# First block rearranged: modulation sums in one PSUM bank, bundled state products, attention in steps between projections

## The chip, the cores and the metric

The kernel runs on one core of a Trainium2 chip, one program, one launch. The metric is the device time of that core in microseconds (us). Five engines work beside each other, each through its own queue in order: TensorE (PE, and PEld for its weight loads), VectorE (DVE), ScalarE (ACT), GpSimd (POOL) and SyncE (SP), which here only issues DMAs. PSUM is the memory that TensorE writes its sums into, in banks of 128 partitions x 512 floats; SBUF is the working memory.

## What is computed

The first block takes x (256 tokens x 1024) through a mixer with two branches and a mixture of experts; a second block of feed-forward layers, a pooling mixer and an attention follows. The change lies in the first block's mixer, and in the first modulation of the second block:

```python
h = rmsnorm(x, g_mix[l])
proj = h @ w_in[l]                      # 1024 x 5376
aq, ak, av, hq, hf_f, hf_b, hi, hg, gate_a, gate_b = jnp.split(proj, SPLIT_POINTS, axis=-1)
attn_o = bidir_gqa(aq, ak, av, q_norm[l], k_norm[l])      # 8 heads of 64, 2 key heads, softmax over 256
hgrn_o = hgrn2_bidir(hq, hf_f, hf_b, hi, hg, lbs_f[l], lbs_b[l], hgrn_norm[l])
merged = (jax.nn.sigmoid(gate_a) * (attn_o @ w_attn_branch[l])
          + jax.nn.sigmoid(gate_b) * (hgrn_o @ w_hgrn_branch[l]))
x = x + merged @ w_out[l]
h = rmsnorm(x, g_ffn[l])
x = x + hier_moe(h, ...)                # 32 experts
...
# hgrn2: q = silu(hq)*scale; f = lb + (1-lb)*sigmoid(z); k = (1-lb)*sigmoid(-z); log_f = log(f)
#   in chunks of 32 tokens, both directions:  S_t = diag(f_t) S_{t-1} + k_t v_t^T ; o_t = S_t^T q_t
# second block: mod = silu(c) @ ada_w[i] + ada_b[i]  gives shift, scale and gate of each sublayer
```

## The kernel before, in words

All data is float32. A large product is made of three matmuls of a shorter float format: each operand is split into a rounded part (`hi`) and the rest (`lo`), and `mm3` (L147 to L150) adds hi*hi, hi*lo and lo*hi into one PSUM bank. `split_w` (L154) splits weights: a cast on ScalarE (L159), a subtraction on VectorE (L160), per 128 x 1024 piece. `gemm_nat` makes a product with tokens on the partitions, in two token blocks `tb` of 128; `gemm_T` (L490) makes it with features on the partitions, in two halves `hp`, and each half is evacuated when its bank is done.

The order of the first block in the source: load x and the gain `g_mix`; normalise a token block (L356), transpose it into `hT` (L360 to L362), project query, key and value (`gemm_nat`); norm and rotary embedding; attention for two token blocks (L430 to L465): per key head g the scores (L440), the row maximum (L443), the exponential with its row sum (L448), transposes (L452), a VectorE copy (L454), the product with v (L458), and at the end the division by the row sum (L463). Then the transposed projections of q and the two gates f (`gemm_T`, evacuated by sigmoids straight from PSUM, L505 to L517), v and the output gate (`gemm_nat`), the recurrence (`hgrn`, from L553: cumulated logarithms, exponentials L569 to L579, products of the chunks, the state chain on VectorE L618, and per state two matmuls into the output, L625), four projections for the branch gates, transposes of both branches' outputs (`to_T`, L347 to L349), the branch products (weights loaded at L664), `w_out`, the router, the experts (L918 on).

The modulation sums of the second block's first two sublayers are made here: `ada_steps` with the engine `pe`, 8 rows of 512 columns. A row's 8 matmuls (L202) put four partial sums on four groups of 32 partitions of a PSUM bank; ScalarE copies the bank (L209), four matmuls against a column of ones add the partials up (L221), VectorE adds the bias (L224).

A scheduler of the framework sets the order on each engine's queue from the program order and its own estimate of durations; `tc.issue_after(x)` keeps a piece behind the instruction x. So the order on a queue is not the source's order. The experts' weights go through SBUF buffers `wgu`, `wdn` (left side) and `xgu`, `xdn` (right side, in pools that take up memory which the first block gives back); SP issues each load when its buffer comes free (L815).

## Time and profile before

| | before |
|---|---|
| device time, median of 3 runs | 1753.44 us (1751.01 to 1757.42) |
| the profiled execution's own time | 1751.05 us |
| its span | 1749.3 us |
| mean granted clock of TensorE | 0.959 |
| TensorE busy | 1569.7 us (90%) |
| VectorE busy | 935.5 us (53%) |
| ScalarE busy | 632.1 us (36%) |
| HBM traffic over the span | 269 GB/s |

The span is the profiled stretch from the first to the last instruction; what lies around it is the difference to the execution's own time. Busy shares are means over the whole span. The first block takes about the first 312 us of it, the experts run to about 756 us, the second block to the end. The granted clock is a share of full speed: 1.00 is the 2.4 GHz level, 0.50 the 1.2 GHz level.

### The profile page before, as it was taken

The page shows a single profiled execution, that of the slowest core. Times are in us where ns is not written, and L with a number is a line of the kernel's source. Part 1 is how long each engine was busy: PE and PEld are TensorE (multiplying, and loading weights), DVE is VectorE, ACT ScalarE, POOL GpSimd, SP SyncE. Part 2 cuts the span into 40 slices and gives each one's busy share as a digit, 9 for nine tenths or more (in the row PEclk, how much of TensorE's full clock was granted, in tenths as well). Part 3 has the DMA queues.
Part 4 walks back from the last instruction along what each step waited for, and adds up shares of the span by engine and source line. Part 5 has one row for each costly group of instructions (what it writes and reads, how often), then busy time and mean ns, then how long its engine had stood idle before and what let it go on. Part 6 is the DMA issues. An engine that isn't in the chain of part 4 may idle for free.

```text
span 1749.3 us, 25202 instructions
## 1 busy us (share of the span) xinstructions
PE 1569.7 (90%) x10307; PEld 1185.4 (68%) x10307; DVE 935.5 (53%) x1620; ACT 632.1 (36%) x1044; POOL 48.9 (3%) x55
## 2 busy tenths in 40 slices
PE   5999998978676778769999899999999999999998
PEld 4875676633223333238999779997999867779997
DVE  4754665312101101037887667778687768765563
ACT  3664444101001000035444444345443456555342
POOL 1100100000000000000000000000000010000000
PEclk8999999899888999889999999999999999999999
DMA  6478475799999999997987467986798565466540
GB/s 199 135 245 295 169 271 213 299 419 420 420 421 377 417 420 421 420 390 266 330 286 259 157 206 252 311 265 209 257 309 282 168 207 178 142 211 216 177 150 25
DMA packets 201727, 472.87 MB, mean 270 GB/s; under 512 B 12712, under 2 KB 105480, under 8 KB 177032
## 3 DMA queue, kind: packets, MB, share of 16 engines
q1 hardware_dynamic: 201608, 471.21, 73.9%
q8 instruction: 83, 1.36, 0.3%
q14 instruction: 36, 0.29, 0.0%
HBM read 470.13 MB, written 1.05 MB: 269 GB/s over the span
## 4 chain that ended last, share of the span: by engine, by line
PE 50%; DMA 10%; DVE 4%; issue 1%; POOL 1%; ACT 1%; SPq 0%; POOLq 0%; DVEq 0%; ACTq 0%
PE ps_g L148 10%; PE ps_g L150 10%; PE ps_g L149 9%; DMA wgu<-in_w_exp_up_dram 5%; PE ps_acc L148 5%; PE ps_acc L150 5%; PE ps_acc L149 5%; DMA xdn<-in_w_exp_down_dram 2%; DMA xgu<-in_w_exp_up_dram 1%; DMA wdn<-in_w_exp_down_dram 1%; PE ps_g L953 1%; POOL rs L137 1%; PE ps_m L221 1%; PE ps_m L1446 1%; DVE rt L1057 1%
## 5 line engine op out<-in xcount | busy, mean ns | idle before, releaser
L148 PE MATMUL ps_g<-hh,hi 128*128 128x256 f32 x1024 | 293.4, 286 | 0.0
L149 PE MATMUL ps_g<-hl,hi 128*128 128x256 f32 x1024 | 289.6, 283 | 0.0
L150 PE MATMUL ps_g<-hh,fl 128*128 128x256 f32 x1024 | 289.1, 282 | 0.0
L1105 DVE TENSOR_TENSOR fl<-fw,hi 128x1024 fp32r<-128x1024 f32 x176 | 211.4, 1219 | 44.2 <-ACT hi L1104 35.2
L1104 ACT CAST hi<-fw 128x1024 fp32r<-128x1024 f32 x176 | 176.8, 1045 | 116.9 <-PE ps_g L149 79.3
L149 PEld LDWEIGHTS ps_g<-hl,hi 128*128 128x128 f32 x1024 | 194.4, 190 | 3.6 <-issue 2.4
L148 PEld LDWEIGHTS ps_g<-hh,hi 128*128 128x128 f32 x1024 | 193.2, 189 | 2.9 <-issue 1.7
L150 PEld LDWEIGHTS ps_g<-hh,fl 128*128 128x128 f32 x1024 | 193.0, 188 | 0.7 <-issue 0.7
L206 DVE SCALAR_TENSOR_TENSOR ev<-ada,condp,ev 128x512 f32<-128x512 f32 x196 | 146.6, 748 | 5.2 <-DMA ada<-in_ada_w_dram 2.2
L150 PE MATMUL ps_acc<-hi,hd 128*128 128x512 f32 x352 | 139.4, 398 | 0.0
L148 PE MATMUL ps_acc<-hi,hd 128*128 128x512 f32 x352 | 138.5, 397 | 0.5 <-ACT hd L1126 0.5
L149 PE MATMUL ps_acc<-fl,hd 128*128 128x512 f32 x352 | 138.3, 394 | 0.0
L918 PE MATMUL ps_g<-wgu,xg 128*32 128x256 f32 x1280 | 91.7, 426 | 41.3 <-DMA wgu<-in_w_exp_up_dram 41.3
L923 DVE TENSOR_TENSOR sq<-sg,ps_g 128x128 f32<-128x128 f32 x32 | 11.9, 373 | 197.1 <-ACT sg L921 197.1
L921 ACT ACTIVATE sg<-ps_g 128x128 f32<-128x128 f32 x32 | 8.9, 278 | 299.8 <-PE ps_g L918 299.8
L160 DVE TENSOR_TENSOR fl<-fw,hi 128x1024 fp32r<-128x1024 f32 x88 | 104.9, 1220 | 20.5 <-ACT hi L159 20.1
L159 ACT CAST hi<-fw 128x1024 fp32r<-128x1024 f32 x88 | 88.6, 1046 | 71.7 <-PE ps_acc L150 69.5
L918 PEld LDWEIGHTS ps_g<-wgu,xg 128*32 128x32 f32 x1280 | 45.7, 121 | 88.0 <-issue 70.5
L148 PE MATMUL ps_g<-hi,hh 128*128 128x512 f32 x240 | 98.0, 409 | 1.4 <-ACT hh L1050 1.2
L150 PE MATMUL ps_g<-hi,hl 128*128 128x512 f32 x240 | 96.7, 404 | 0.0
L953 PE MATMUL ps_g<-wdn,hid 128*32 128x512 f32 x320 | 90.2, 631 | 6.4 <-DVE sq L923 6.4
L957 PE MATMUL ps_acc<-part,ohT 128*128 128x512 f32 x128 | 65.2, 633 | 22.1 <-ACT part L955 12.7
(405 smaller groups left out, 2721.5 us busy)
## 6 DMA issues: line engine op xcount, KB each, us to landing
fw<-in_ffn_w_in_dram SPq DMA_DIRECT2D x88, 1024.0 KB, 7.8
ada<-in_ada_w_dram SPq DMA_DIRECT2D x112, 512.0 KB, 4.8
fw<-in_ffn_w_out_dram SPq DMA_DIRECT2D x44, 1024.0 KB, 6.9
wgu<-in_w_exp_gate_dram SPq DMA_DIRECT2D x40, 1024.0 KB, 19.9
wgu<-in_w_exp_up_dram SPq DMA_DIRECT2D x40, 1024.0 KB, 9.1
wdn<-in_w_exp_down_dram SPq DMA_DIRECT2D x40, 1024.0 KB, 19.8
xgu<-in_w_exp_gate_dram SPq DMA_DIRECT2D x24, 1024.0 KB, 19.9
xgu<-in_w_exp_up_dram SPq DMA_DIRECT2D x24, 1024.0 KB, 7.8
```

What stands on the lines that cost most here:

```text
L137: lead["gp"] = gp.tensor_tensor(out=r, in0=ms, in1=mhalf[:, :n], op=ALU.pow)
L148: pe.matmul(o, ah, bh, start=start, stop=False)
L149: pe.matmul(o, ah, bl, start=False, stop=False)
L150: pe.matmul(o, al, bh, start=False, stop=stop)
L159: lead["hi"] = act.copy(out=hi, in_=w)
L160: lead["lo"] = dve.tensor_tensor(out=lo, in0=w, in1=f32(hi), op=ALU.subtract)
L206: eng.scalar_tensor_tensor(out=o, in0=wk, scalar=ck, in1=o, op0=ALU.mult, op1=ALU.add)
L918: pe.matmul(up[32 * j:32 * j + 32], xg[:, k, s0:s0 + CAP], w[k // 4][:, :, k % 4, j * P:j * P + P], start=k == 0, stop=k == 7)
L953: pe.matmul(o[r_:r_ + 32], hid[i][:, 32 * j:32 * j + 32], wd[i][q][:, jj, c_], start=jj == 0, stop=jj == 1)
L957: pe.matmul(acc[tb][h], ohT[:, tb], part[:, c_], start=e == 0, stop=e == NE - 2)
L1104: act.copy(out=hi, in_=w[:, k_])
L1105: dve.tensor_tensor(out=lo_[:, k_], in0=w[:, k_], in1=f32(hi), op=ALU.subtract)
```

## The change

- The gain `g_mix` is loaded as one row of 4 KB, and two matmuls with a row of ones spread it over the partitions of two PSUM banks; `xn` reads it there.
- The scaling of the router gain `gq` is put inside `issue_after(wr)`, behind the router weights.
- The first modulation sums get a function of their own, `ada_first`: the columns of `condp` are shifted so that row r of eight lands on partition r of each group of 32; all 64 matmuls add into one bank, then one copy, four matmuls with 8 columns (`sel` adds the four groups up), eight additions of the bias.
- Attention is cut into five steps, `attend(tb, g)` and `weigh(tb)`, which `some` issues between the halves of the transposed projections. p is divided by its row sum before it is transposed; the copy of the transposed p is on ScalarE; the product has v as the stationary operand, so that the output comes feature major (`AO`), and no transposes are needed before the branch product. The branch weights of attention come in four loads of 64 partitions.
- The transposed projections are evacuated by plain copies, in the order f forward, q, f backward; sigmoids and logarithms follow from SBUF, the logarithm takes its affine part as scale and bias.
- The state products of the recurrence are issued in two bundles per chain, after the third and the seventh state.
- Buffers: one more `lo`, one more `w2`; `AQ` and `AK` move into `x_sb`, so the pool on the right side shrinks from 24 KB to 20 KB a partition.

The core of the diff:

```diff
-            lo = spl.tile([P, 1024], F32R, tag="lo", name="lo", bufs=4)
+            lo = spl.tile([P, 1024], F32R, tag="lo", name="lo", bufs=5)
...
+    def ada_first(new_w, new_ev):
+        src = io["ada_w_2"][0].rearrange("(k p) n -> p k n", p=P)
+        sums = []
+        def row(r):
+            sl, c, h = r // 4, r // 2 % 2, r % 2
+            n0 = (sl * 3 + c) * D + 512 * h
+            w = [new_w() for _ in range(2)]
+            for q in range(2):
+                sp.dma_start(out=w[q], in_=src[:, 4 * q:4 * q + 4, n0:n0 + 512])
+            if r == 0:
+                sums.append(ps("m", 512))
+            for k in range(8):
+                j = k % 4
+                pe.matmul(sums[0][32 * j:32 * j + 32], condp[:, k, 7 - r:39 - r], w[k // 4][:, j],
+                          start=r == 0 and k < 4, stop=r == 7 and k >= 4, skip_group_check=True)
+        def end():
+            ev = new_ev("ev")
+            act.copy(out=ev, in_=sums[0])
+            sel = small(32, "sel")
+            dve.tensor_reduce(out=sel, in_=ident.rearrange("p (j r) -> p r j", j=4), axis=AX.X, op=ALU.add)
+            o = ps("t", 4, 8)
+            for m in range(4):
+                pe.matmul(o[:, m], ev[:, m * P:m * P + P], sel[:, 0:8], start=True, stop=True)
+            for sl in range(2):
+                for c in range(2):
+                    for h in range(2):
+                        b0 = (sl * 3 + c) * 8 + 4 * h
+                        dst = ab_dst(sl, c, h)
+                        r = 4 * sl + 2 * c + h
+                        dve.tensor_tensor(out=dst[:, :, None], in0=o[:, :, r:r + 1], in1=colB[:, 0, b0:b0 + 4][:, :, None], op=ALU.add)
+                ab_gain(sl, mods[sl][:, 0], 0, 8)
+        return [lambda r=r: row(r) for r in range(8)] + [end]
...
+    g_row = x_sb[0:1, 1, :]
+    sp.dma_start(out=g_row, in_=io["g_mix"][0:1])
...
-    NW2 = 8
+    NW2 = 9
...
-    sp.dma_start(out=gmix, in_=io["g_mix"][0:1].to_broadcast([P, D]))
...
+    gmix = [ps("acc", 512) for _ in range(2)]
+    for h in range(2):
+        pe.matmul(gmix[h], ones[0:1], g_row[:, 512 * h:512 * h + 512], start=True, stop=True)
...
-    AQ = [par.tile([P, 512], F32, name=f"AQ{i}") for i in range(2)]
-    AK = par.tile([P, 512], F32, name="AK")
+    AQ = [x_sb[:, 0, 512 * i:512 * i + 512] for i in range(2)]
+    AK = x_sb[:, 1, 0:512]
+    AO = x_sb[:, 0].rearrange("p (j t) -> p j t", t=S)
...
+    def attend(tb, g):
         t_ = slice(tb * P, tb * P + P)
-        rs = small(8, "arow")
-        po = ps("m", 8, 64)
-        for g in range(2):
-            sc = [ps("acc", 2, S) for _ in range(2)]
+        sc = [ps("acc", 2, S) for _ in range(2)]
+        for i in range(2):
+            for u in range(2):
+                h_ = slice(64 * u, 64 * u + 64)
+                pe.matmul(sc[u][:, i], QT[g][h_, i, t_], KT_[h_, g], start=True, stop=True)
+        for u in range(2):
+            mx = small(2, "amx")
+            dve.reduce_max(out=mx, in_=sc[u], axis=AX.X)
+            dve.tensor_scalar(out=mx, in0=mx, scalar1=-0.125, scalar2=None, op0=ALU.mult)
+            pt = w3("pt")
+            rs = small(2, "arow")
             for i in range(2):
-                for u in range(2):
-                    h_ = slice(64 * u, 64 * u + 64)
-                    pe.matmul(sc[u][:, i], QT[g][h_, i, t_], KT_[h_, g], start=True, stop=True)
-            for u in range(2):
-                mx = small(2, "amx")
-                dve.reduce_max(out=mx, in_=sc[u], axis=AX.X)
-                dve.tensor_scalar(out=mx, in0=mx, scalar1=-0.125, scalar2=None, op0=ALU.mult)
-                pt = w3("pt")
-                for i in range(2):
-                    h = 4 * g + 2 * i + u
-                    act.activation(out=pt[:, S * i:S * i + S], in_=sc[u][:, i], func=AF.Exp, scale=0.125,
-                                   bias=mx[:, i:i + 1], accum_out=rs[:, h:h + 1])
-                tt = ps("t", 4, P)
-                for j in range(4):
-                    pe.transpose(tt[:, j], pt[:, j * P:j * P + P], ident)
-                pT = w3("pT")
-                dve.tensor_copy(pT, tt.rearrange("p a b -> p (a b)"))
-                for i in range(2):
-                    h = 4 * g + 2 * i + u
-                    for kb in range(2):
-                        pe.matmul(po[:, h], v2(pT, P)[:, 2 * i + kb], vA[:, kb, g * 64:g * 64 + 64],
-                                  start=kb == 0, stop=kb == 1)
-        ri = small(8, "ari")
-        dve.reciprocal(out=ri, in_=rs)
-        ao = AQ[tb]
-        dve.tensor_tensor(out=v2(ao, 64), in0=po, in1=ri[:, :, None].to_broadcast([P, 8, 64]), op=ALU.mult)
-        dump(f"ao{tb}", ao)
-        AO.append(ao)
+                act.activation(out=pt[:, S * i:S * i + S], in_=sc[u][:, i], func=AF.Exp, scale=0.125,
+                               bias=mx[:, i:i + 1], accum_out=rs[:, i:i + 1])
+            dve.reciprocal(out=rs, in_=rs)
+            dve.tensor_tensor(out=v2(pt, S), in0=v2(pt, S), in1=rs[:, :, None].to_broadcast([P, 2, S]), op=ALU.mult)
+            tt = ps("t", 4, P)
+            for j in range(4):
+                pe.transpose(tt[:, j], pt[:, j * P:j * P + P], ident)
+            pT = w3("pT")
+            act.copy(out=pT, in_=tt.rearrange("p a b -> p (a b)"))
+            pTs[tb, g, u] = pT.rearrange("p (i b t) -> p i b t", i=2, t=P)
+    def weigh(tb):
+        po = ps("acc", 4, P)
+        for u in range(2):
+            for kb in range(2):
+                for g in range(2):
+                    pe.matmul(po[64 * g:64 * g + 64].rearrange("p (i u) t -> p u i t", u=2)[:, u], vA[:, kb, g * 64:g * 64 + 64],
+                              pTs[tb, g, u][:, :, kb], start=kb == 0, stop=kb == 1)
+        t_ = slice(tb * P, tb * P + P)
+        act.copy(out=AO[:, :, t_], in_=po)
+    att_todo = [lambda: attend(0, 0), lambda: attend(0, 1), lambda: (weigh(0), attend(1, 0)),
+                lambda: attend(1, 1), lambda: weigh(1)]
...
+            act.copy(out=dst[hp], in_=o.rearrange("p a b -> p (a b)"))
+            between()
...
+    def func_f(d, hp):
+        act.activation(out=Ks[d][hp], in_=Fs[d][hp], func=AF.Sigmoid, scale=-1.0)
+        act.activation(out=Fs[d][hp], in_=Fs[d][hp], func=AF.Sigmoid)
...
+            act.activation(out=Fs[d][hp][:, c_], in_=Fs[d][hp][:, c_], func=AF.Ln, scale=omlb[:, d, h:h + 1],
+                           bias=lbt[:, d, h:h + 1])
...
+    gemm_T(load_in(1280, 512), Fs[0], lambda: some(1, 0))
+    gemm_T(load_in(768, 512), Qs, lambda: some(1, 1))
+    gemm_T(load_in(1792, 512), Fs[1], lambda: some(1, 1))
+    some(9, 0)
+    for hp in range(2):
+        func_q(hp)
+        for d in range(2):
+            func_f(d, hp)
...
+                if j not in (2, 6):
+                    continue
                 for i in range(2):
-                    c0 = S * i + 32 * n2
-                    pe.matmul(O[32 * r2:32 * r2 + 32, tb2, i], b[:, c0:c0 + 32], STt[:, j, i],
-                              start=False, stop=(d == 1 and j == 6 and i == 1), skip_group_check=True)
+                    for jj in range(done, j + 1):
+                        n2 = order[jj + 1]
+                        tb2, r2 = n2 // 4, n2 % 4
+                        c0 = S * i + 32 * n2
+                        pe.matmul(O[32 * r2:32 * r2 + 32, tb2, i], b[:, c0:c0 + 32], STt[:, jj, i],
+                                  start=False, stop=(d == 1 and jj == 6 and i == 1), skip_group_check=True)
+                done = j + 1
...
-    for tb in range(2):
-        to_T(AO[tb], aoT, 4, tb, ["t"])
+    act.copy(out=aoT[0], in_=AO)
+    dve.tensor_tensor(out=aoT[1], in0=AO, in1=f32(aoT[0]), op=ALU.subtract)
...
+            for g in range(2):
+                sp.dma_start(out=w[64 * g:64 * g + 64], in_=io[wn][0, 256 * g:256 * g + 256].rearrange("(j d) n -> d j n", d=64)[:, 2 * h:2 * h + 2])
...
-    dve.tensor_scalar(out=gq, in0=gq, scalar1=float(D) ** 0.5, scalar2=None, op0=ALU.mult)
     lead["wr"] = dve.tensor_tensor(out=wr, in0=wr, in1=gcol[:, :, None].to_broadcast([P, 8, 36]), op=ALU.mult)
     iom = prt.tile([P, 32], F32, name="iom")
     with tc.issue_after(lead["wr"].ins):
+        dve.tensor_scalar(out=gq, in0=gq, scalar1=float(D) ** 0.5, scalar2=None, op0=ALU.mult)
```

VectorE at the start of the program, before (`xn` are the normalised rows of a token block, `hTl` the small part of their transpose, `lo` that of the weights, `ms` a mean square):

```order
L135 TENSOR_SCALAR ms<-ss 128x1
L356 SCALAR_TENSOR_TENSOR xn<-x_in,rs,W_96 128x512 x2
L362 TENSOR_TENSOR hTl<-ps_acc,hTh 128x4x128 x2
L160 TENSOR_TENSOR lo<-w_in,hi 128x1024 x2
L135 TENSOR_SCALAR ms<-ss 128x1
L686 TENSOR_SCALAR gq<-gq 128x8
L356 SCALAR_TENSOR_TENSOR xn<-x_in,rs,W_96 128x512 x2
L160 TENSOR_TENSOR lo<-w_in,hi 128x1024
L362 TENSOR_TENSOR hTl<-ps_acc,hTh 128x4x128 x2
```

and of the changed kernel:

```order
L216 TENSOR_REDUCE sel<-K 128x32
L135 TENSOR_SCALAR ms<-ss 128x1
L397 SCALAR_TENSOR_TENSOR xn<-x_in,rs,ps_acc 128x512 x2
L403 TENSOR_TENSOR hTl<-ps_acc,hTh 128x4x128 x2
L160 TENSOR_TENSOR lo<-w_in,hi 128x1024 x2
L135 TENSOR_SCALAR ms<-ss 128x1
L397 SCALAR_TENSOR_TENSOR xn<-x_in,rs,ps_acc 128x512 x2
L160 TENSOR_TENSOR lo<-w_in,hi 128x1024
L403 TENSOR_TENSOR hTl<-ps_acc,hTh 128x4x128 x2
```

The scaling of `gq` no longer stands between the mean square of the second token block and its `xn`; a small reduction for `sel` stands at the very front.

ScalarE in the attention, before (L448 is the exponential, L505 the sigmoid of q, L159 the cast of weights):

```order
L448 ACTIVATE W_98,arow<-ps_acc,amx 128x256 x14
L505 ACT_TABLE_LOAD
L505 ACTIVATE sgq<-ps_g 128x512
L448 ACT_TABLE_LOAD
L448 ACTIVATE W_98,arow<-ps_acc,amx 128x256 x2
L159 CAST hi<-w_in 128x1024 x3
L505 ACT_TABLE_LOAD
L505 ACTIVATE sgq<-ps_g 128x512
L487 ACTIVATE sg_584<-colA 128x8
L159 CAST hi<-w_in 128x1024
```

and of the changed kernel, in a stretch of its attention (L490 is the exponential, L571 the logarithm, L498 the copy of the transposed p, L549 the evacuation of a projection, L563 the sigmoid of q):

```order
L571 ACTIVATE W_96<-W_96,lbt,omlb 128x256
L490 ACT_TABLE_LOAD
L490 ACTIVATE W_98,arow<-ps_acc,amx 128x256 x2
L571 ACT_TABLE_LOAD
L571 ACTIVATE W_96<-W_96,lbt,omlb 128x256
L490 ACT_TABLE_LOAD
L490 ACTIVATE W_98,arow<-ps_acc,amx 128x256 x2
L571 ACT_TABLE_LOAD
L571 ACTIVATE W_96<-W_96,lbt,omlb 128x256
L498 COPY W_98<-ps_t 128x512
L159 CAST hi<-w_in 128x1024 x2
L498 COPY W_97<-ps_t 128x512
```

Fourteen exponentials in a row have become pairs, with logarithms, copies and casts between them, and a table load at each turn from one function to the other.

TensorE in the recurrence, before (L625 is a state product, L148 to L150 a projection that runs between):

```order
L625 MATMUL ps_m<-W_96,b 32x128 x2
L148 MATMUL ps_g<-hi,hTh 128x512
L149 MATMUL ps_g<-lo,hTh 128x512
L150 MATMUL ps_g<-hi,hTl 128x512
L625 MATMUL ps_m<-W_96,b 32x128
L148 MATMUL ps_g<-hi,hTh 128x512
L149 MATMUL ps_g<-lo,hTh 128x512
L625 MATMUL ps_m<-W_96,b 32x128
L150 MATMUL ps_g<-hi,hTl 128x512
L625 MATMUL ps_m<-W_96,b 32x128
L148 MATMUL ps_g<-hi,hTh 128x512
```

and of the changed kernel (L687 is the state product):

```order
L687 MATMUL ps_m<-W_97,b 32x128
L148 MATMUL ps_g<-hi,hTh 128x512
L149 MATMUL ps_g<-lo,hTh 128x512
L687 MATMUL ps_m<-W_97,b 32x128
L150 MATMUL ps_g<-hi,hTl 128x512
L148 MATMUL ps_g<-hi,hTh 128x512
L687 MATMUL ps_m<-W_97,b 32x128
L149 MATMUL ps_g<-lo,hTh 128x512
L150 MATMUL ps_g<-hi,hTl 128x512
L148 MATMUL ps_g<-hi,hTh 128x512
L687 MATMUL ps_m<-W_97,b 32x128 x5
```

The products still go one by one between the matmuls of a projection, but for the last five of a chain.

## Rows read from the trace of the kernel before

**Rows 1.** The page: busy us of each engine, share of the span, instructions.

```profile
PE 1569.7 (90%) x10307; PEld 1185.4 (68%) x10307; DVE 935.5 (53%) x1620; ACT 632.1 (36%) x1044; POOL 48.9 (3%) x55
```

**Rows 2.** Stretches: length, busy of PE, PEld, DVE, ACT, POOL, clock, DMA share, GB/s.

```profile
57.00:81.00 24.00, 22.43 (x178) 19.50 (x178) 16.58 (x32) 15.82 (x41) 0.00 (x0) 1.00 0.10 28
81.00:103.00 22.00, 22.00 (x184) 21.72 (x184) 16.20 (x43) 19.91 (x28) 0.00 (x0) 1.00 0.77 277
...
340.00:756.00 416.00, 305.58 (x2541) 132.02 (x2540) 53.44 (x175) 26.11 (x67) 0.00 (x0) 0.90 1.00 415
```

**Rows 3.** VectorE's start: start, duration, instruction, in brackets idle before and releaser.

```profile
8.76 1.42 DVE L356 SCALAR_TENSOR_TENSOR xn<-x_in,rs,W 128x512 f32<-128x512 f32 x2 [2.88 <-DMA W<-in_g_mix_dram]
...
15.42 0.14 DVE L135 TENSOR_SCALAR ms<-ss 128x1 f32<-128x1 f32 x1
26.73 0.17 DVE L686 TENSOR_SCALAR gq<-gq 128x8 f32<-128x8 f32 x1 [11.17 <-DMA gq<-in_g_ffn_dram]
26.81 1.42 DVE L356 SCALAR_TENSOR_TENSOR xn<-x_in,rs,W 128x512 f32<-128x512 f32 x2
```

**Rows 4.** TensorE's start, same columns.

```profile
18.36 0.40 PE L149 MATMUL ps_g<-lo,hTh 128*128 128x512 f32 x1
27.62 1.97 PE L360 MATMUL ps_acc<-K,xn 128*128 128x128 f32 x8 [8.86 <-DVE xn L356]
...
46.59 0.36 PE L148 MATMUL ps_g<-hTh,hi 128*128 128x256 f32 x1
```

**Rows 5.** SyncE's DMA issues at the start: start, duration, line, target and source.

```profile
23.77 0.43 SPq L644 DMA_DIRECT2D gq<-in_g_ffn_dram  x1
24.31 29.73 SPq L310 DMA_DIRECT2D w_in<-in_w_in_dram  x6
```

**Rows 6.** DMA issues by target: count, KB each, median us from issue to landing.

```profile
w_in<-in_w_in_dram SPq DMA_DIRECT2D x19, 1024.0 KB, 5.0
```

**Rows 7.** Two stretches at half clock, columns as in Rows 2.

```profile
21.70:31.90 10.20, 4.28 (x14) 3.75 (x15) 4.98 (x7) 2.21 (x4) 0.00 (x0) 0.50 0.50 124
...
182.10:185.50 3.40, 3.40 (x10) 2.66 (x9) 3.40 (x5) 3.36 (x5) 0.00 (x0) 0.50 0.03 5
```

**Rows 8.** Groups by line and shape, 46-300 us: busy us, mean ns, idle.

```profile
L202 PE MATMUL ps_m<-W,condp 128*32 128x512 f32 x128 | 17.5, 625 | 0.6 <-DMA W<-in_ada_w_dram 0.3 <-DVE AB L224 0.3
...
L221 PE MATMUL ps_m<-ones,ev 128*128 128x1 f32 x64 | 7.8, 243 | 1.3 <-ACT ev L209 1.2
...
L458 PE MATMUL ps_m<-W,W 128*128 128x64 f32 x64 | 8.6, 278 | 0.3 <-DVE W L454 0.3
...
L625 PE MATMUL ps_m<-W,b 128*32 128x128 f32 x112 | 13.4, 280 | 1.1 <-DVE W L615 1.1
...
L448 ACT ACTIVATE W<-ps_acc,amx 128x256 f32<-128x256 f32 x16 | 7.4, 474 | 5.1 <-DVE amx L444 5.1
...
L569 ACT ACT_TABLE_LOAD x3 | 3.8, 1283 | 0.1
```

**Rows 9.** TensorE around one group of modulation sums.

```profile
106.42 0.95 PE L221 MATMUL ps_m<-ones,ev 128*128 128x1 f32 x8
107.23 0.48 PE L149 MATMUL ps_g<-lo,hTh 128*128 128x512 f32 x1
```

**Rows 10.** TensorE after a wait, and at the transposes of attention's output.

```profile
181.52 0.47 PE L148 MATMUL ps_g<-hi,hTh 128*128 128x512 f32 x1 [2.35 <-ACT Et L572]
...
238.50 0.60 PE L347 MATMUL ps_t<-K,AQ 128*128 128x128 f32 x4
240.33 0.50 PE L148 MATMUL ps_g<-hi,bhTh 128*128 128x512 f32 x1 [1.23 <-ACT bhTh L348]
```

**Rows 11.** Around the first expert matmul: two stretches, and the matmul.

```profile
310.00:320.00 10.00, 10.00 (x81) 6.30 (x81) 1.15 (x8) 2.68 (x7) 0.00 (x0) 0.57 0.66 256
...
330.00:340.00 10.00, 9.58 (x60) 3.57 (x59) 2.40 (x8) 0.86 (x2) 0.00 (x0) 1.00 0.46 164
...
311.82 1.06 PE L918 MATMUL ps_g<-wgu,xg 128*32 128x256 f32 x2
```

More of the change, by code (lines that the diff above doesn't have):

```diff
@@ L20 @@
 EPS = 1e-6
-NA = (0, 0, 6, 3, 8, 0)
 HGRN_SCALE = 128 ** -0.5
@@ L181, in tile_model, with ab_dst, ab_gain, ada_steps @@
     mods = {}
-    def ada_steps(sl, what, new_ev, tag, new_w, nk, eng):
+    def ab_dst(sl, c, h):
+        if sl not in mods:
+            mods[sl] = sm.tile([P, 2, 8], F32, tag="AB", name="AB", bufs=3)
+        return mods[sl][:, 1 - c, 4 * h:4 * h + 4]
+    def ab_gain(sl, dst, h, n):
+        g0 = 24 + sl * 8 + 4 * h
+        dve.scalar_tensor_tensor(out=dst, in0=dst, scalar=1.0, in1=colA[:, g0:g0 + n], op0=ALU.add, op1=ALU.mult)
+    def ada_first(new_w, new_ev):
[30 more added lines that the diff above has]
+        return [lambda r=r: row(r) for r in range(8)] + [end]
+    def ada_steps(sl, what, new_ev, tag, new_w, nk):
         i, s = sl // 3, sl % 3
@@ L195, in row @@
             if k0 == 0:
-                part[c, h] = ps(tag, 512) if eng is pe else new_ev("ev")
+                part[c, h] = new_ev("ev")
             o = part[c, h]
             for k in range(k0, k0 + nk):
-                wk, ck = w[:, k - k0], condp[:, k, 0:1]
-                if eng is pe:
-                    j = k % 4
-                    pe.matmul(o[32 * j:32 * j + 32], condp[:, k], wk, start=k < 4, stop=k >= 4)
-                elif k == 0:
-                    eng.tensor_scalar(out=o, in0=wk, scalar1=ck, scalar2=None, op0=ALU.mult)
-                else:
-                    eng.scalar_tensor_tensor(out=o, in0=wk, scalar=ck, in1=o, op0=ALU.mult, op1=ALU.add)
-            if eng is pe and k0 + nk == 8:
-                part[c, h] = new_ev("ev")
-                act.copy(out=part[c, h], in_=o)
+                wk, ck = w[:, k - k0], condp[:, k, 7:8]
+                if k == 0:
+                    dve.tensor_scalar(out=o, in0=wk, scalar1=ck, scalar2=None, op0=ALU.mult)
+                else:
+                    dve.scalar_tensor_tensor(out=o, in0=wk, scalar=ck, in1=o, op0=ALU.mult, op1=ALU.add)
         def row_steps(c, h):
@@ L222, in ab @@
             b0 = (s * 3 + c) * 8 + 4 * h
[L223 removed]
             dve.tensor_tensor(out=dst, in0=o2, in1=colB[:, i, b0:b0 + 4], op=ALU.add)
             if c == 1:
[L226 to L227 removed]
+                ab_gain(sl, dst, h, 4)
         def gate(h):
@@ L246, in ada_steps @@
             end = (lambda c=c, h=h: ab(c, h)) if what == "ab" else (lambda h=h: gate(h))
-            if eng is pe:
-                rs[-1] = lambda f=rs[-1], g=end: (f(), g())
-            elif last:
+            if last:
                 rs[0] = lambda f=rs[0], g=last: (g(), f())
@@ L253, in ada_steps @@
             last = end
-        return st if eng is pe else st + [last]
+        return st + [last]
     phT = ExitStack()
@@ L487, in tile_model, with gemm_T @@
     act.activation(out=sg8, in_=colA[:, 16:24], func=AF.Sigmoid)
-    dve.tensor_tensor(out=condp[:, :, 0], in0=sg8, in1=colA[:, 16:24], op=ALU.mult)
-    def gemm_T(w, evac):
+    dve.tensor_tensor(out=condp[:, :, 7], in0=sg8, in1=colA[:, 16:24], op=ALU.mult)
+    def gemm_T(w, dst, between):
         sw = [split_w(spl, v[:, k:k + 2]) for v in w for k in range(0, 4, 2)]
@@ L525, in ada_w, with some @@
         return Wq[3][:, 4 * ada_n[0]:4 * ada_n[0] + 4]
-    ada_todo = [st for sl in range(2) for st in ada_steps(sl, "ab", wsg, "m", ada_w, 4, pe)]
-    def ada_some(n):
-        for st in ada_todo[:n]:
-            st()
-        del ada_todo[:n]
-    gemm_T(load_in(768, 512), ev_q)
-    ada_some(NA[0])
-    gemm_T(load_in(1280, 512), ev_f(0))
-    ada_some(NA[1])
-    gemm_T(load_in(1792, 512), ev_f(1))
-    ada_some(NA[2])
-    gemm_nat(spl, per_tb(hT), load_in(2304, 512), lambda tb, o: act.copy(out=Vs[tb], in_=o))
-    ada_some(NA[3])
+    ada_todo = ada_first(ada_w, wsg)
+    def some(n_att, n_ada):
+        for todo, n in ((att_todo, n_att), (ada_todo, n_ada)):
+            for st in todo[:n]:
+                st()
+            del todo[:n]
+    gemm_T(load_in(1280, 512), Fs[0], lambda: some(1, 0))
[6 more added lines that the diff above has]
+            func_f(d, hp)
+    gemm_nat(spl, per_tb(hT), load_in(2304, 512), lambda tb, o: (act.copy(out=Vs[tb], in_=o), some(0, 1)))
     def ev_hg(tb, o):
@@ L548, in ev_hg @@
         dve.tensor_tensor(out=v2(HGs[tb], P), in0=v2(sg, P), in1=hgn[:, None, :].to_broadcast([P, 4, P]), op=ALU.mult)
+        some(0, 1)
     gemm_nat(spl, per_tb(hT), load_in(2816, 512), ev_hg)
-    ada_some(NA[4])
+    some(0, 9)
+    for hp in range(2):
+        for d in range(2):
+            logs(d, hp)
     HO = [W1[12 + tb] for tb in range(2)]
@@ L558, in tile_model @@
             Ft, Kt, Qt = Fs[d][hp], Ks[d][hp], Qs[hp]
-            act.activation(out=Ft, in_=Ft, func=AF.Ln)
             b = w2("b")
@@ L611, in tile_model @@
                               start=True, stop=True)
+            done = 0
             for j, n in enumerate(order[:7]):
```

56 lines of the change are left out of this document (22 added, 34 removed).

## The prediction

> **What bounds the kernel now.** I read the page first. TensorE is busy for nine tenths of the span [rows 1], so time is gained where TensorE works less, or waits less. The chain of waits is of no use for the first block: followed back from the end it runs into the expert weights' transfers and stays there. So I read the first block by stretches. From 340 to 756 us the DMA share is 1.00 at 415 GB/s [rows 2]: the experts are bound by their weights, and those loads follow one another from the point at which the first block gives up its memory. The instructions behind the first expert matmul stand in the same order before and after. So what the first block saves passes on whole, if the loads start as much earlier.
>
> In the first block TensorE is nearly full. From 57 to 81 us, the attention, it works 22.43 of 24.00 us; from 81 to 103 us it works all 22.00 and ScalarE 19.91 [rows 2]. The one large hole is at the start: VectorE idles 11.17 us in front of the scaling of `gq`, a router gain of 8 columns that nobody needs for another 270 us; its DMA is issued only at 23.77 [rows 3, 5]. VectorE is in order, so the second block of normalised rows, `xn`, stands behind it at 26.81. TensorE's transposes of `xn` start at 27.62 after an idle of 8.86 us [rows 4]. The granted clock is 0.50, the 1.2 GHz level, from 21.70 to 31.90 [rows 7]: the engine fell to it while idle, and climbed back after working again.
>
> **The change, part by part.**
>
> *The start.* `gq` is now scaled behind the router weights, and is gone from the start of VectorE's queue. `xn` then waits only for its own mean square, done at 15.42+0.14 [rows 3], and the power behind it. That is over 10 us earlier, so the transposes can follow the matmuls that end after 18.36. The idle of 8.86 goes. In the half-clock stretch TensorE works 4.28 us [rows 7]; at full clock that is 2.14, so 2.1 more go. The first `xn` waited 2.88 us for the 512 KB of `g_mix` [rows 3]; 4 KB and two matmuls replace it, but the first projection also waits for its weights, so I count 0.5, between 0 and 2.9. Sum −11.5. Next late is the following pair of `w_in` loads: SP issues them at 24.31 [rows 5], behind the same row of small DMAs as before, and one lands in 5.0 us [rows 6]. With cast and subtraction, and two loads sharing the bandwidth, they are ready between about 31 and 36. TensorE would arrive there at 46.59−11.5 = 35.1 [rows 4]. So the floor just about touches: ends −13 and −6.
>
> *Modulation sums.* The matmuls on the weights stay: 64 instructions, 17.5 us [rows 8]. Before, each of eight rows has its own copy and four one-column matmuls. One such group holds TensorE from 106.42 to 107.23, 0.81 us [rows 9]; all of them are busy 7.8 us and wait 1.3 [rows 8]. Seven of eight groups go: (7.8+1.3)×7/8 = 8.0 us, less a wider last group and one wait for the single copy: −7.5, ends −6 and −8.5. Seven ScalarE copies go too; they weigh nothing here.
>
> *Attention output.* Thirty-two instructions (64 records, 8.6 us [rows 8]) become 16 of 64 output partitions × 256 columns. The trace has none of this shape. The nearest is the modulation matmul: 0.27 us for 512 columns with four groups of 32 output columns running side by side, so about 1.09 alone, 0.55 for 256 columns. Sixteen cost 8.7 us alone and 4.4 in pairs. Between 0 and −4.2 I take −2, the middle, since the rows show side-by-side running but not for this width. The outputs come out feature major, so eight transposes at 238.50 go, with their wait of 1.23 before 240.33 [rows 10]: −2, ends −1.5 and −2.3. A cast and a subtraction of 128x1024 take their place; they lie under projections.
>
> *State products.* Both kernels issue 56 matmuls of 32 output columns (13.4 us, 0.24 each [rows 8]). The source bundles them, but the scheduler spreads them again: 28 runs before, 28 after, only the last of each chain a run of five. If five ran like the modulation groups, four at a time, 20 to 25 of the 56 would lose two thirds: −4. If a run stalls on its latest state, +2. I take −1.
>
> *Attention in steps.* This is the cost. Each step is scores, maximum, exponential on ScalarE, now a scaling on VectorE, transposes, and a copy that moves to ScalarE. Before, 14 of the 16 exponentials (0.474 us each [rows 8]) follow one another on ScalarE. Now evacuations, casts, sigmoids and logarithms stand between them, and the kernel has 36 table loads instead of 26. TensorE has a half projection to run meanwhile, but its order is fixed too: transposes of p stand at a set place between matmuls. One step's chain is two exponentials, a table load of 1.283 [rows 8] and a scaling, about 3 us, against some 5 us of matmuls in a half projection. I estimate 8 steps × 1 us of wait, less the 1.6 us that the stretch waits today (24.00−22.43): +6. Ends 0 (all hidden) and +19 (the ten new loads, 12.8 us, on the path besides).
>
> The row on the table loads shows three of them with 0.1 us of idle before [rows 8], so a load costs its 1.283 us there and little more. The Trainium skill, "ScalarE: Activation LUTs", section "What ACT_TABLE_LOAD costs", adds a drain of about 1380 ns to each switch, 2.66 us in all. By it the ten loads would be 26.6 us of ScalarE, and the ScalarE rival below would end at +10 instead of −4. No row here shows that drain as time in which ScalarE stands still, so the sum goes by 1.283.
>
> *Memory.* The pool on the right shrinks from 24 to 20 KB a partition, the left ones grow, and three expert loads of 1 MB that could start before the first block ended must now wait for its last reads. Three MB at 415 GB/s are 7.6 us. But behind the first block the queue is not full: its share is 0.66 from 310 to 320 and 0.46 from 330 to 340 [rows 11], 8.8 us of idle in which they fit. I take 0, with +7.6 as the far end. The branch weights in half-partition loads: 0, they come a projection ahead, at most +2.
>
> Sum: −11.5 −7.5 −2 −2 −1 +6 = −18. I add 1 for waits in the rearranged recurrence that I could not place: −17. The profiled execution took 1751.05, its span 1749.3 and 1.75 around it; 1751.05−17 = 1734. The median of the runs is 2.4 above the profiled one, so 1736.
>
> **Rivals.**
> - *ScalarE becomes the bound.* It is busy 19.91 of 22.00 us in the stretch from 81 to 103 [rows 2], and gets ten loads. For it: this fullness. Against it: 57 to 81 has room, 15.8 of 24 us busy. All ten on the path: −17+12.8, so 1749.
> - *The start gives half.* The pair of `w_in` loads, issued at 24.31, holds TensorE back: −6 for −11.5, so 1742. For it: their issue does not move in the order. Against it: 5.0 us to landing.
> - *The prefetch is missed.* The idle of the queue is not where the three loads fall: +7.6, so 1744.
> - *Slower.* Every softmax step stalls TensorE for the whole 3 us chain, and each stall is followed by a stretch at half clock. The trace has this once: a wait of 2.35 us before 181.52 [rows 10], and the granted clock at 0.50 from 182.10 to 185.50 [rows 7], which costs half of 3.4 us. Eight times (3+1.7) is 38 against −23 from the other terms: +15, so 1768. It decides against the change above 23/8 = 2.9 us for a step. Against it: the matmuls of half a projection stand between the steps.
> - *More than forecast.* Attention hides whole, pairs and bundles run side by side: −17−6−2−3 = −28, so 1725.
> - *It does not do what it says.* For the bundles this is already in the sum. For `gq` the order shows the move.
>
> **How the numbers follow.** Forecast 0.54; more 0.14; ScalarE 0.10; half a start 0.09; prefetch 0.07; slower 0.06. A change under 0.5%, 8.8 us, is one that a measurement of this kernel can hardly tell from none; 1744.7 is that border. Faster: 0.53+0.14+0.07 (half a start)+0.05 (prefetch)+0.01 = 0.80. Same: 0.01+0.09+0.02+0.02 = 0.14. Slower: 0.06. The range, 1722 to 1750, takes in ScalarE's case and the bulk of the larger gain; left out are the slower case and the far ends of the terms. The likeliest case alone spans 1728 to 1743.
>
> **What would show it.** Right: `xn` of the second block before 18 us, no half clock between 20 and 32, the first transposed projection at 33 to 36 us instead of 46.59; one group of four matmuls on the modulation sums; no transposes ahead of the branches; the first expert matmul about 17 us earlier than 311.82 [rows 11], and the DMA share at 1.00 from about 323. Wrong: waits of TensorE on ScalarE over 3 us in the attention, half clock there, or expert loads that saturate no earlier than now.

## The result, and the profile after

The changed kernel takes 1735.17 us (median of 4 runs, 1734.3 to 1736.8) against 1753.97 for the kernel before (4 runs, 1751.01 to 1757.42): a ratio of 0.9893, 95% interval 0.9873 to 0.9913. Forecast were 1736 and a range of 1722 to 1750. The profiled execution has a span of 1733.6 us and took 1735.33; the span fell by 15.7 us.

The first `xn` of each token block on VectorE (start, duration, instruction, in brackets the idle time before and what ended it), to be read against [rows 3]:

```profile
6.79 0.75 DVE L397 SCALAR_TENSOR_TENSOR xn<-x_in,rs,ps_acc 128x512 f32<-128x512 f32 x1 [1.06 <-PE ps_acc L390]
15.12 1.41 DVE L397 SCALAR_TENSOR_TENSOR xn<-x_in,rs,ps_acc 128x512 f32<-128x512 f32 x2 [0.74 <-POOL rs L137]
```

TensorE there, against [rows 4]:

```profile
17.08 0.39 PE L149 MATMUL ps_g<-lo,hTh 128*128 128x512 f32 x1
17.31 0.60 PE L401 MATMUL ps_acc<-K,xn 128*128 128x128 f32 x4
...
33.08 0.36 PE L148 MATMUL ps_g<-hTh,hi 128*128 128x256 f32 x1
```

The second `xn` runs at 15.12 instead of 26.81, its transposes follow the matmuls of the first token block without a pause, and the first transposed projection starts at 33.08 instead of 46.59. The clock does not fall; the stretch of the change answers to the first of [rows 7] (length; busy us of PE, PEld, DVE, ACT, POOL; clock; DMA share; GB/s):

```profile
20.00:32.00 12.00, 12.00 (x73) 10.54 (x72) 9.29 (x15) 6.10 (x11) 2.04 (x1) 1.00 0.87 267
```

Four of the groups of TensorE from 33 to 285 us, which answer to [rows 8] (busy us, mean ns | idle before):

```profile
L209 PE MATMUL ps_m<-W,condp 128*32 128x512 f32 x128 | 17.9, 619 | 0.0
L687 PE MATMUL ps_m<-W,b 128*32 128x128 f32 x112 | 13.1, 292 | 3.8 <-DVE W L673 3.6 <-DVE W L676 0.2
L507 PE MATMUL ps_acc<-W,W 128*64 128x256 f32 x16 | 5.7, 498 | 0.0
L219 PE MATMUL ps_t<-sel,ev 128*128 128x8 f32 x8 | 1.0, 245 | 0.0
```

The modulation matmuls cost what they did; the groups behind them fell from 7.8 to 1.0 us. The attention is where the profile got worse. TensorE waits four times before transposes of p, 8.4 us in all (the rows between them are left out):

```profile
55.93 0.63 PE L496 MATMUL ps_t<-K,W 128*128 128x128 f32 x4 [2.02 <-DVE omlb L533]
74.80 0.63 PE L496 MATMUL ps_t<-K,W 128*128 128x128 f32 x4 [0.58 <-DVE W L493]
80.41 0.66 PE L496 MATMUL ps_t<-K,W 128*128 128x128 f32 x4 [3.56 <-ACT W L498]
94.79 0.65 PE L496 MATMUL ps_t<-K,W 128*128 128x128 f32 x4 [2.20 <-ACT W L498]
```

In the kernel before, the same transposes waited 1.3 us in all:

```profile
L452 PE MATMUL ps_t<-K,W 128*128 128x128 f32 x32 | 5.1, 276 | 1.3 <-ACT W L448 1.3
```

The wait of 2.02 us is put down to a small VectorE instruction that stands right behind the scaling of p; the exponentials of that p had stood behind a sigmoid and its two table loads (50.50 to 53.74 on ScalarE). Half clock follows the two longest waits, for part of these stretches:

```profile
80.40:84.00 3.60, 3.59 (x20) 2.64 (x20) 2.46 (x3) 3.60 (x5) 0.00 (x0) 0.68 0.63 189
94.80:99.00 4.20, 4.20 (x22) 2.44 (x22) 1.48 (x3) 4.17 (x7) 1.27 (x1) 0.59 0.16 58
```

A third stretch at half clock, 40.77 to 44.18, follows a wait of 2.04 us for the rotary embedding, which is not the softmax. What ScalarE does ahead of the wait of 3.56 us:

```profile
70.79 0.60 ACT L571 ACTIVATE W<-W,lbt,omlb 128x256 f32<-128x256 f32 x1
71.41 1.28 ACT L490 ACT_TABLE_LOAD   x1
72.71 0.48 ACT L490 ACTIVATE W<-ps_acc,amx 128x256 f32<-128x256 f32 x1
...
73.75 1.28 ACT L571 ACT_TABLE_LOAD   x1
75.04 0.60 ACT L571 ACTIVATE W<-W,lbt,omlb 128x256 f32<-128x256 f32 x1
75.66 1.28 ACT L490 ACT_TABLE_LOAD   x1
...
79.29 0.60 ACT L571 ACTIVATE W<-W,lbt,omlb 128x256 f32<-128x256 f32 x1
79.80 0.56 ACT L498 COPY W<-ps_t 128x512 f32<-128x512 f32 x1
```

Two exponentials, a table load, one logarithm, a table load, two exponentials: each of these logarithms of 0.60 us costs two loads of 1.28. The copy at 79.80, for which TensorE waits, is queued behind them. From 69.5 to 80.4 us ScalarE is full, TensorE is not:

```profile
69.50:80.40 10.90, 6.77 (x54) 5.38 (x47) 5.59 (x11) 10.77 (x18) 0.00 (x0) 1.00 0.55 192
```

At the end of the first block, against [rows 11], the first expert matmul and the transfers around it:

```profile
296.75 1.06 PE L982 MATMUL ps_g<-wgu,xg 128*32 128x256 f32 x2
```

```profile
310.00:320.00 10.00, 10.00 (x102) 5.21 (x101) 5.11 (x23) 2.40 (x6) 0.00 (x0) 1.00 0.59 244
320.00:330.00 10.00, 9.58 (x119) 4.52 (x121) 1.39 (x3) 0.28 (x1) 0.00 (x0) 1.00 0.99 387
```

The first expert matmul comes 15.1 us earlier, and the DMA share is back near 1.00 from 320 us instead of 340.

The span's 15.7 us by five marks on TensorE (start of the instruction, us):

| mark | before | after | change within the stretch up to it |
|---|---|---|---|
| first transposed projection | 46.59 | 33.08 | −13.5 |
| first matmul of the v projection | 105.39 | 107.86 | +16.0 |
| first matmul of the branches | 240.33 | 224.74 | −18.1 |
| first expert matmul | 311.82 | 296.75 | +0.5 |
| end of the span | 1749.3 | 1733.6 | −0.6 |

The second and third rows mix something: ahead of the v projection stand 28 modulation matmuls now (56 records in the trace, two to an instruction), 8 before (16 records). Twenty of them at 17.9/64 = 0.28 us are 5.6. So the stretch with the attention lost 10.4 us, and the one with the recurrence won 12.5. The two stretches before, then after (columns as above):

```profile
46.59:105.39 58.80, 55.46 (x446) 49.81 (x445) 43.05 (x99) 42.42 (x82) 3.32 (x4) 1.00 0.43 147
105.39:240.33 134.94, 127.07 (x776) 83.29 (x773) 76.20 (x140) 63.24 (x82) 12.92 (x9) 0.97 0.68 235
33.08:107.86 74.78, 64.12 (x455) 49.27 (x453) 44.72 (x100) 62.31 (x111) 6.45 (x5) 0.93 0.61 209
107.86:224.74 116.88, 112.10 (x678) 72.61 (x674) 68.63 (x128) 62.52 (x77) 7.32 (x7) 0.99 0.61 199
```

With the attention, TensorE's idle grew from 3.3 to 10.7 us, and the mean clock fell from 1.00 to 0.93; 0.07 of 74.78 us is an estimate of 5.2 us for that. With the recurrence, the idle fell from 7.9 to 4.8 us.

### The profile page after: what moved, and what is told of

Its sections match the earlier page's. It is cut to its first block, busy times and chain, and to the rows that moved or that the text cites. A ratio compares the mean times of both kernels' runs of the same rounds, so it can differ in the third digit from the quotient of the medians.

```text
span 1733.6 us, 25012 instructions
## 1 busy us (share of the span) xinstructions
PE 1558.9 (90%) x10215; PEld 1167.8 (67%) x10215; DVE 932.0 (54%) x1614; ACT 650.6 (38%) x1066; POOL 47.4 (3%) x55
## 4 chain that ended last, share of the span: by engine, by line
PE 49%; DMA 12%; DVE 4%; issue 1%; POOL 1%; ACT 1%; SPq 0%; POOLq 0%; DVEq 0%; ACTq 0%
PE ps_g L150 10%; PE ps_g L148 10%; PE ps_g L149 9%; DMA wgu<-in_w_exp_up_dram 6%; PE ps_acc L148 5%; PE ps_acc L149 5%; PE ps_acc L150 5%; DMA xdn<-in_w_exp_down_dram 2%; DMA wdn<-in_w_exp_down_dram 1%; DMA xgu<-in_w_exp_up_dram 1%; DMA xgu<-in_w_exp_gate_dram 1%; POOL rs L137 1%; PE ps_m L1510 1%; PE ps_m L261 1%; DMA fw<-in_ffn_w_in_dram 1%
## 5 line engine op out<-in xcount | busy, mean ns | idle before, releaser
L148 PE MATMUL ps_g<-hh,hi 128*128 128x256 f32 x1024 | 292.0, 285 | 0.0
L150 PE MATMUL ps_g<-hh,fl 128*128 128x256 f32 x1024 | 289.1, 282 | 0.0
L150 PEld LDWEIGHTS ps_g<-hh,fl 128*128 128x128 f32 x1024 | 196.1, 192 | 0.7 <-issue 0.7
L148 PEld LDWEIGHTS ps_g<-hh,hi 128*128 128x128 f32 x1024 | 192.5, 188 | 2.9 <-issue 1.7
L150 PE MATMUL ps_acc<-hi,hd 128*128 128x512 f32 x352 | 139.1, 398 | 0.0
L148 PE MATMUL ps_acc<-hi,hd 128*128 128x512 f32 x352 | 138.2, 396 | 0.5 <-ACT hd L1190 0.5
L159 ACT CAST hi<-fw 128x1024 fp32r<-128x1024 f32 x88 | 88.6, 1045 | 71.0 <-PE ps_acc L150 68.8
L148 PE MATMUL ps_g<-hi,hh 128*128 128x512 f32 x240 | 97.3, 407 | 1.3 <-ACT hh L1114 1.2
L150 PE MATMUL ps_g<-hi,hl 128*128 128x512 f32 x240 | 96.8, 404 | 0.0
```

The costliest lines, as they stand in the source:

```text
L148: pe.matmul(o, ah, bh, start=start, stop=False)
L150: pe.matmul(o, al, bh, start=False, stop=stop)
L159: lead["hi"] = act.copy(out=hi, in_=w)
```

## Experiments

Each is compared with runs of the kernel before on the same chip; the ratio is the recorded estimate with its interval, not the quotient of the two medians. The changed kernel was timed apart from them, next to a kernel before of 1753.97, so a difference from its 1735.17 carries up to 2 us of difference between the medians of the kernel before.

**e1, only `gq` moved in the kernel before.**

```diff
-    dve.tensor_scalar(out=gq, ...)
     with tc.issue_after(lead["wr"].ins):
+        dve.tensor_scalar(out=gq, ...)
```

> The kernel before, with one edit: the scaling of gq stands behind the router weights. The order on TensorE is that of the kernel before. Theory (the start's gain is the stall on gq): TensorE's idle of 8.86 us before the second transposes and the half-clock stretch behind it go; the first transposed projection starts 11 us earlier (35 to 36 instead of 46.59), and all of it arrives at the end: 1743, 10 to 12 us under the kernel before. Rival (the start's gain comes from the 512 KB of g_mix and the earlier loads): the w_in loads at about 24 us hold the projection back, and only 4 to 6 us come through: 1749.

Measured: 1743.08 against 1751.84, ratio 0.9951 (0.9935 to 0.9968). The second `xn` and its transposes in it:

```profile
15.86 1.42 DVE L356 SCALAR_TENSOR_TENSOR xn<-x_in,rs,W 128x512 f32<-128x512 f32 x2 [0.74 <-POOL rs L137]
```

```profile
18.41 1.33 PE L360 MATMUL ps_acc<-K,xn 128*128 128x128 f32 x8
```

The first transposed projection starts at 35.66, 10.9 us earlier, as the theory had it; of these 8.8 arrive in the median, where the theory had 10 to 12, and 9.4 at the first expert matmul (302.41). One moved instruction is about half of the whole change.

**e9, the same edit undone in the changed kernel.**

```diff
+    dve.tensor_scalar(out=gq, ...)
     lead["wr"] = ...
     with tc.issue_after(lead["wr"].ins):
-        dve.tensor_scalar(out=gq, ...)
```

> The changed kernel, with the scaling of gq back in its old place: it stands again between the second mean square and xn on VectorE; nothing else is edited. Theory (the start's gain is this stall, in the changed kernel too): xn waits for the gain's DMA, issued at about 22 us, TensorE idles 8 to 10 us before the second transposes and falls to half clock: 9 to 11 us over the changed kernel, 1745. Rival (the shorter queue of DMAs at the start, with no 512 KB for g_mix, is most of the gain): at most 4 us over it, 1739.

Measured: 1744.09 against 1752.84, ratio 0.9955 (0.9939 to 0.9972); 8.9 us above the changed kernel's median. VectorE and TensorE in it:

```profile
25.08 0.17 DVE L750 TENSOR_SCALAR gq<-gq 128x8 f32<-128x8 f32 x1 [10.94 <-DMA gq<-in_g_ffn_dram]
```

```profile
26.05 1.09 PE L401 MATMUL ps_acc<-K,xn 128*128 128x128 f32 x4 [8.63 <-DVE xn L397]
```

The shorter DMA queue at the start does not shorten this wait. The theory stands, from both sides.

**e2, only the modulation sums, in the kernel before.** `ada_first` replaces the list of steps, with three, two and the other rows after three projections.

```diff
-    ada_todo = [st for sl in range(2) for st in ada_steps(sl, "ab", wsg, "m", ada_w, 4, pe)]
+    ada_todo = ada_first(ada_w, wsg)
-NA = (0, 0, 6, 3, 8, 0)
+NA = (0, 0, 3, 2, 9, 0)
```

> The kernel before, with the first modulation sums alone made as in the changed kernel: one bank, one copy, one group of four matmuls. Theory: seven groups of 0.9 us go from a stretch where TensorE is full: 7 to 8 us under the kernel before, 1746. Rival: the groups stood in stretches where TensorE waits for the recurrence anyway, and the saving turns into longer waits there: 0 to 3 us, 1752.

Measured: 1766.88 against 1751.84, ratio 1.0099 (1.0078 to 1.0121): slower, which neither theory had. TensorE's wait for the rows' weights from 100 to 235 us (total, times, longest), a stretch that begins with the first of these waits, and the state products:

```profile
PE ps_m L209 <- DMA W<-in_ada_w_dram: 9.4, 5, 2.7
```

```profile
140.30:164.20 23.90, 15.15 (x61) 5.70 (x62) 2.43 (x12) 2.58 (x3) 0.00 (x0) 0.50 0.92 329
```

```profile
L673 PE MATMUL ps_m<-W,b 128*32 128x128 f32 x112 | 20.5, 283 | 3.4 <-DVE W L663 3.4
```

The last three rows stand in one run of 24 matmuls on TensorE's queue, and everything behind them waits for their weights; from the first of these waits on the clock is at half for 23.9 us. Besides, the state products stand in 48 runs instead of 28 and are busy for 20.5 us instead of 13.4. In the kernel before, three and a half rows are issued at the same place of the source, and on the queue they stand half a row at a time between other matmuls. That the copies between the rows held them apart there is how I read the two orders; no run tests it alone.

**e5, the same with the rows spread.** Behind the first three, the rows come one to a projection. The last of them are loaded into memory that the first branch gate also uses, so the gate's values are overwritten; the instructions are the same.

```diff
-NA = (0, 0, 3, 2, 9, 0)
+NA = (0, 0, 3, 1, 1, 1)
```

> As e2, the kernel before with the first modulation sums in one bank, but with its rows spread one to a projection up to the second branch gate, so that no two rows' matmuls follow one another on TensorE without a projection between. Theory (the sums are worth 8 us of TensorE; e2 lost because TensorE stood in line for the rows' weights, 2.7 us a pair): waits on the modulation weights under 2 us together, 5 to 9 us under the kernel before: 1745. Rival (the single bank itself costs, by its longer hold or its late end): not under 1752.

Measured: 1745.79 against 1753.3, ratio 0.9964 (0.9951 to 0.9976). TensorE waits nowhere from 100 to 235 us for the modulation weights; it waits 8.9 us for the recurrence's scaled operands, and its state products, in longer runs, are busy for 9.1 us instead of 13.4. The total is what the theory said; but three things moved, so the 8 us of the sums are shown by their own rows (7.8 busy and 1.3 idle before, 1.0 and 0.0 after), not by this run alone.

**e3, logarithms behind the attention.**

```diff
-                act.activation(out=pt[...], ..., func=AF.Exp, ...)
+                lead["exp"] = act.activation(out=pt[...], ..., func=AF.Exp, ...)
...
-    for hp in range(2):
-        for d in range(2):
-            logs(d, hp)
+    with tc.issue_after(lead["exp"].ins):      # the last exponential of attention
+        for hp in range(2):
+            for d in range(2):
+                logs(d, hp)
```

> The changed kernel, with the eight logarithms queued on ScalarE behind the last exponential of attention. Theory (attention's extra cost is the table loads between exponentials and logarithms): the waits of 0.58, 3.56 and 2.20 us of TensorE before transposes of p, between 73 and 95 us, shrink by 4 to 6 us together: 1730. Rival (the steps' own chain of maximum, exponential, scaling, transposes, copy is the cost, or the recurrence that hangs on the logarithms comes late): the waits stay or move behind: 1735, not under 1734.

Measured: 1727.05 against 1751.84, ratio 0.9865 (0.9849 to 0.9882); 8 us under the changed kernel, 6 when each is set against the kernel before that was timed next to it; 4 to 6 were expected. The stretch from the first transposed projection to the v projection, which answers to 33.08:107.86 above:

```profile
32.81:99.34 66.53, 60.19 (x454) 46.44 (x453) 43.00 (x98) 55.94 (x104) 5.16 (x4) 1.00 0.69 238
```

It is 8.3 us shorter. TensorE's idle is 6.3 us instead of 10.7, and the clock is full throughout, which the estimate above puts at 5.2; the two are some 1 us more than the stretch gained. Of its waits from 33 to 100 us, the one for the copy of p is 1.1 us instead of 5.8, and the one of 2.0 at the first transposes stays:

```profile
PE ps_t L496 <- DVE omlb L533: 2.0, 1, 2.0
PE ps_t L496 <- ACT W L498: 1.1, 1, 1.1
```

The first expert matmul is at 289.04, 7.7 earlier than in the changed kernel: the saving in the attention passes on nearly whole. The kernel has 35 table loads, one fewer than the changed kernel's 36: what changed is what stands behind them.

**e6, sigmoids too.**

```diff
+    with tc.issue_after(lead["exp"].ins):
         for hp in range(2):
             func_q(hp)
             ...func_f(d, hp)
     ... and the logarithms as in e3
```

> The changed kernel, with the sigmoids of the transposed projections and the logarithms queued on ScalarE behind the last exponential of attention; 29 table loads instead of 36 (35 in e3). Theory (ScalarE's loads between exponentials are the cost of the steps): at or under e3, 1724 to 1728. Rival (the recurrence then starts too late and TensorE waits for it): 1730 or more, with new waits of TensorE between 100 and 160 us.

Measured: 1724.69 against 1753.3, ratio 0.9849 (0.9828 to 0.987), the fastest of all with e10. The first expert matmul is at 285.70. The longest of what is left of TensorE's waits from 33 to 98 us name VectorE, not ScalarE:

```profile
PE ps_t L466 <- DVE W L434: 2.0, 1, 2.0
PE ps_t L496 <- DVE arow L492: 1.7, 1, 1.7
```

**e7, the copy of the transposed p on VectorE.**

```diff
-            act.copy(out=pT, in_=tt.rearrange("p a b -> p (a b)"))
+            dve.tensor_copy(pT, tt.rearrange("p a b -> p (a b)"))
```

> The changed kernel, with the copy of the transposed p on VectorE as in the kernel before. Theory (the logarithms' table loads are the cost; the copies only stand behind them): TensorE's waits for the copies go, those for the exponentials stay, 2 to 4 us under the changed kernel: 1732. Rival (moving eight copies of 0.58 us to ScalarE is the cost): as much as e3, 1727.

Measured: 1732.52 against 1753.3, ratio 0.9888 (0.9869 to 0.9907), not to be told from the changed kernel's 0.9893, though the median is 2.6 us lower. The first expert matmul is at 297.23, no earlier. The waits for the copy are gone, and those for the scaling of p grew from 0.6 to 3.6 us; below them the stretch up to the v projection:

```profile
PE ps_t L496 <- DVE W L493: 3.6, 2, 1.9
```

```profile
33.32:108.52 75.20, 66.71 (x454) 50.36 (x452) 47.92 (x107) 61.56 (x104) 6.46 (x5) 0.91 0.60 208
```

L493 is the scaling of p behind the exponentials: more than half of the lateness was the exponential's, not the copy's. TensorE's idle fell from 10.7 to 8.5 us, about as the theory had it, but the mean clock is 0.91 instead of 0.93, and the stretch is no shorter (75.20 against 74.78). The rival falls; of the theory's 2 to 4 us the marks show none.

**e8, all attention steps ahead of the projections; e10, with e6 besides.**

```diff
+    some(9, 0)
     gemm_T(load_in(1280, 512), Fs[0], lambda: some(1, 0))
```

> The changed kernel, with all five attention steps issued ahead of the transposed projections in the source; 30 table loads. Theory (what the steps cost is the company they keep on ScalarE, not that they are steps): the logarithms come after the exponentials by themselves, so near e3: 1726 to 1731. Rival (the steps between projections are what hides the softmax): TensorE waits 5 us more in the attention than in the changed kernel: 1740.

> The changed kernel, with the attention steps ahead of the transposed projections in the source and the sigmoids and logarithms behind the last exponential: e6 and e8 together, 30 table loads. Theory (once ScalarE does not change tables between exponentials, the place of the steps does not matter): 1723 to 1727, as e6 and e8 alone. Rival (the two savings add, 10.5 and 8.6 us): 1717.

Measured: 1726.55 against 1753.3, ratio 0.9859 (0.984 to 0.9878), and 1724.85 against 1752.84, ratio 0.9836 (0.9813 to 0.9858). Cutting the attention into steps between projections is not what hides the softmax: with the steps up front the order on the engines mixes them by itself, and the logarithms come late; TensorE's waits before transposes of p are 1.6 us in e8 instead of 8.4. The savings of e6 and e8 do not add.

**e4, state products unbundled.**

```diff
-                if j not in (2, 6):
-                    continue
                 for i in range(2):
-                    for jj in range(done, j + 1):
-                        ...
+                    ...one product, for state j
```

> The changed kernel, with the state products issued state by state as before. TensorE's order is the same up to the recurrence; there the products stand in 48 runs instead of 28. Theory of the prediction (bundling is worth about 1 us): 1 to 3 us over the changed kernel, 1737. Rival (the 6 us that the stretch with the recurrence gained beyond the modulation sums come from the bundles): 5 to 6 us over it, 1741.

Measured: 1744.37 against 1751.84, ratio 0.9956 (0.9942 to 0.997); 9.2 us above the changed kernel, more than either theory had. The products from 33 to 300 us, and the stretch from the v projection to the branches, which answers to 107.86:224.74 above:

```profile
L683 PE MATMUL ps_m<-W,b 128*32 128x128 f32 x112 | 20.7, 282 | 3.8 <-DVE W L673 3.6 <-DVE W L676 0.2
```

```profile
109.21:235.60 126.39, 121.28 (x679) 75.42 (x675) 68.72 (x128) 62.64 (x77) 7.48 (x7) 1.00 0.56 184
```

The same 112 records take 20.7 us instead of 13.1, with the same waits, and the stretch is 9.5 us longer at a clock that is no lower. 1.4 us are lost already ahead of the v projection, where the two kernels' orders agree. In the changed kernel a lone product (two records) keeps the next matmul 0.33 us away, a run of five (ten records) 0.55, so 0.11 for each:

```profile
221.27 0.41 PE L687 MATMUL ps_m<-W,b 128*32 128x128 f32 x2
221.60 0.50 PE L149 MATMUL ps_g<-lo,hTh 128*128 128x512 f32 x1
...
222.50 0.62 PE L687 MATMUL ps_m<-W,b 128*32 128x128 f32 x10
223.05 0.50 PE L149 MATMUL ps_g<-lo,hTh 128*128 128x512 f32 x1
```

## Why the prediction was right

The total was right to a microsecond, and that is in part luck: the start and the recurrence gave more than forecast, the attention cost more, and the errors balanced each other. The span fell by 15.7 us where 17 were forecast.

- *The start*: forecast −11.5, measured −13.5. The stall on `gq` is 10.9 (e1) of it; the rest I put down to `g_mix`, 1.2 us already at the first projection's matmul (11.98 instead of 13.16). The floor that I feared did not touch: the next loads of `w_in` are issued at 22.47, and the buffers for the following ones are free earlier too.
- *Modulation sums*: −7.5, measured 6.8 busy and 1.3 idle, −8.1. What I had not seen is that the place of the rows on the queue matters as much: in e2, where three of them stand together, the kernel is 15 us slower, with 9.4 us of waits for their weights, half clock behind and scattered state products. In the changed kernel the rows lie apart and do not wait.
- *Attention output*: −2 for the side-by-side products. The two halves of a pair start within 7 to 10 ns of each other (below), so they do run together. At full clock a pair starts 0.22 us after the last (66.78 and 67.00), and sixteen would be 3.5, below the better end of 4.4; half of them ran at half clock here. Most of the −2 for the transposes did not come: the other branch's transposes and their cast took the place, 0.74 us of wait, and the stretch from there to the experts is 0.5 longer. "A wait of 1.23 goes" was true, and a like one was next late.
- *State products*: −1 against the kernel before; 13.4 became 13.1, and their waits grew from 1.1 to 3.8. That hid the point. In the kernel before, half of the products stood in runs of 14, 7, 4 and 3, which the source does not ask for; e2 and e4, without the bundles, have no run longer than two. The changed kernel has six runs of five and two of three on its queue, and e4 shows that the bundling keeps 9 us. That a product in a run of five costs a third of a lone one is what the prediction's better end had.
- *Attention in steps*: +6, less 2 for the products, forecast +4; measured +10.4. This is the step that was mis-sized, and not in the sum of its waits: eight times 1 us were forecast before transposes of p, and they are 8.4. What the sum put at nothing is the half clock, worth 5.2 by the estimate above; it stood only in the slower rival. The shape was wrong too: four waits instead of eight, and 6.3 of the 8.4 us stand behind logarithms and the table loads around them, which e3 and e8 bear out. Two of the waits are followed by half clock, the mechanism of the slower rival, at two places instead of eight. Waits of TensorE over 3 us and half clock in the attention were the prediction's own signs of being wrong, and both are there. Of the ScalarE rival, a full ScalarE holds for 69.5 to 80.4 us. I had the order of those rows before me (logarithm, load, exponential, load) and priced it as an average.
- *The recurrence*: I added 1 for waits that I could not place; the stretch gave 12.5, which is 8.1 for the sums and 4.4 more. The wait of 2.35 us before 181.52 and the half-clock stretch behind it are gone [rows 7, 10]. The prediction said that the trace has such a stretch once; the kernel before has a second one in the recurrence, 151.40 to 154.80, behind a wait of 1.21 us for a sum's copy, and that is gone as well. One new one, 201.19 to 204.61, stands behind a wait of 1.92 us for the state products, so 1.7 us net are won by the clock. That the wait of 2.35 us is gone because the exponentials of the first chain now run before 97 us, long before TensorE needs them, is my reading; no run tests it.
- *Memory*: 0. The three loads moved behind the first block's end and fell into the idle of the queue; the share is at 0.59 from 310 to 320 us even so.

In "ScalarE: Activation LUTs", section "What ACT_TABLE_LOAD costs", the Trainium skill adds about 1380 ns of drain to a switch. Here a logarithm that ends at 71.39 is followed by a load at 71.41 and an exponential at 72.71: 1.32 in all, with no such drain between them. What the loads cost is what stands in line behind them.
